# RWKV-7 and short-convolution mixer: keys too are placed by held GpSimd transfers, and the decayed reads move into the scan

## The chip, the cores and the metric

The kernel runs on one core of one Trainium2 chip. The metric is the device time of one launch, in microseconds (us), as the median over repeated runs. The engines are named as the profile names them: PE is TensorE (matrix products and transposes), DVE is VectorE, ACT is ScalarE, POOL is GpSimd, and SP starts most of the transfers.

## The reference

One layer of a diffusion backbone in fp32 with D_MODEL 2048: 128 context tokens, and 256 latent tokens that start from cached states. Both streams go through the same weights. One input projection `z = h @ w_in` feeds two branches. Branch B is a gated convolution of width 3. Branch A is RWKV-7 time mixing with 32 heads of size 64, in two directions; its scan is what the change touches:

```python
def step(S, inp):
    r_t, w_t, k_t, v_t, a_t, b_t = inp
    sa = jnp.einsum('dbhij,dbhj->dbhi', S, a_t)
    S = S * w_t[..., None, :] + sa[..., :, None] * b_t[..., None, :] + v_t[..., :, None] * k_t[..., None, :]
    y = jnp.einsum('dbhij,dbhj->dbhi', S, r_t)
    return S, y
...
S_fin, ys = _wkv_bidir(S0, _heads(r2), _heads(decay), _heads(k_dir), _heads(v2),
                       _heads(-kk2), _heads(kk2 * a))
y = ys[0] + ys[1]
mu = jnp.mean(y, axis=-1, keepdims=True)
var = jnp.mean(jnp.square(y - mu), axis=-1, keepdims=True)
y = ((y - mu) * lax.rsqrt(var + GN_EPS)).reshape(bsz, t, D_A) * lnx_g + lnx_b
```

A bonus from r, k and v is added, a gate is applied, and the two branches go through their output projections and are merged. Outputs are both token streams and the final context state of each direction.

## The kernel before

**Stages.** A prologue computes the conditioning and the normalised input. A loop over 16 blocks of two heads (128 channels) then runs branch A's scan. A tail projects the gated results out. Matrix products with weights are made in split precision: each weight and each activation is split into a high and a low part (`split`: ACT casts the high part, L88, DVE subtracts it for the low part, L89, named whi_ and wlo_ with a projection's letters), and `mm3` multiplies them in three products (L81 to L83).

**The stream.** The weight projections are cut into units, one `mm3` each with 384 tokens as columns. `Stream` holds them in order, loads their weights ahead, and `ds_.go(n)` puts the next n of them into PE's program. PE's order is exactly that of the code: a step of the scan, so many units, the next step. The numbers that set this are in one line of constants (PB0, PB1, H0, H1, CH0, CH1, WINDOW and others). The order on the other engines is set by a scheduler, which works with its own estimate of when each operand is ready, with priorities (the scan has one 300 higher), and with `issue_after`, which puts an instruction behind another.

**One block**, in the order of the code:

- *prep_b* (L668) makes the decayed keys `bk` (L680, L681) and the decayed reads `pr` (L682 and L685, L687) of the two directions, in tiles of 128 by 6 chunks by 128. After PB0 = 14 units come the masked products `pA` (L708), one burst of 24 small products for each direction, with PB1 = 6 units between; DVE masks them into the tile `A` (L714). GpSimd then multiplies `bk` by the decay of its chunk (L722), and DVE transposes the values v in 32x32 pieces into `vt` (L727). Pieces of A go through DRAM (`ui`, then `un` and `ux`) into a layout in which DVE solves 30 rows of a triangular system (L740, L742), and by `uo` back into A. DVE then transposes two pieces into `x11` (L755); the last of these is `box["turned"]`.
- *finish* of the block before (L948) stands between the PB0 units and the first masked product: PE transposes the normalised output `ytok` into `py`; ACT and DVE scale it, add the bonus and gate it.
- *prep_c* loads the initial state `s_in`. Eight GpSimd transfers (L777) carry `vt` into the lower half of `sav`. Ten PE transposes `pb` (L784) turn `bk`, and four ACT copies (L785) put them into `bt`, with one unit behind each group. Then the bonus's terms and the state's transposes.
- *prep_a* of the next block makes its decay and rates: the weights `lwh`, `lwl`, products `pl`, sigmoids `sig`, and the norm `kn` of its keys, held behind `box["turned"]`. Then the stream is filled up to WINDOW = 80 units (24 more in block 0, 16 more in block 15).
- *scan* starts with `pav` (L862), the corner products `pH` and `pX` with copies back into A and x11 (L890 for pX), and the bonus. Two chains of chunk steps then alternate, with CH0 = 2 units behind each step, CH1 = 4 when one is left. A step is: `po` from the state (L816), which adds to `sav` and `ytok`; `pq` (L833) with its copy into `sav` by ACT (L835); `pu` from `bt` and `sav` (L840), from which DVE writes the new state, by a copy in the first step of chain 0 (L843), by an addition otherwise (L845). At the end `py2` adds the rest of the output to ytok.
- *prep_k* of the next block (reciprocals L651, the product L652, scans L659, Exp of the decay `ep` on ACT L661, and the elementwise steps L664 to L666) is issued at a fixed place inside the scan, held behind two of the pX copies.
- *norm* (L932 to L942) makes the group norm of `ytok` on DVE, with a square on ACT and a power on GpSimd (L941).

Of the kernel before, what the change touches and what calls it, by code (L numbers as in the profile page):

```python
# [56 lines left out]
def hybrid_step(ctx, tc, cst, x_prompt, x_sample, state_f, state_b, c, c_ctx, ada_w, ada_b, norm_g,  # L57
# [613 lines left out]

    def prep_b(b, o):

        r, kk = r_[b], o["kk"]
        o["pr"], o["bk"] = [], []
        for d in range(2):
            ep, em, kd, bn = o["ep"][d], o["em"][d], o["kd"][d], o["bn"][d]
            pr = sp.tile([P, NCH, P], F32, tag=f"pr{d}", name=f"pr_{b}_{d}")
            bk = sp.tile([P, NCH, P], F32, tag=f"bk{d}", name=f"bk_{b}_{d}")
            V.tensor_tensor(bk[:, :, 0:C], c3(bn[:]), c3(em[:]), ALU.mult)  # L680
            V.tensor_tensor(bk[:, :, C:P], c3(kd[:]), c3(em[:]), ALU.mult)  # L681
            V.tensor_tensor(pr[:, :, 0:C], c3(kk[:, ::-1] if d else kk[:]), ep[:, :, 0:C], ALU.mult)  # L682
# [19 lines left out]
        for d in range(2):  # L702
# [7 lines left out]
            for n0, w in ((0, 4), (4, 2)):  # L710
                mk = cs[:, m0:m0 + P].rearrange("p (w t) -> p w t", t=C).unsqueeze(1).broadcast_to([P, w, 2, C])
                for h in range(2):
                    f0 = NCH * d + n0
                    last = V.tensor_tensor(A[:, :, f0:f0 + w, hss[h]].rearrange("p w n t -> p n w t"),  # L714
                                           pas[h, n0][:, 0:w, :].rearrange("p n (w t) -> p n w t", t=C), mk,
                                           ALU.mult).ins
# [4 lines left out]
        for d in range(2):
            G.tensor_tensor(o["bk"][d][:], o["bk"][d][:], o["ep"][d][:, :, C:C + 1].broadcast_to([P, NCH, P]), ALU.mult)  # L722

        vt = sp.tile([P, 2, T], F32, tag="vt", name=f"vt_{b}")
        with tc.issue_after(last):
            for d in range(2):
                V.transpose(vt[:, d], v_[b][:, ::-1] if d else v_[b][:])  # L727
# [25 lines left out]

        for d in range(2):
            box["turned"] = V.transpose(x11[0:32, 12 * d:12 * d + 12, :], blocks(A, d, 0)).ins  # L755

    def prep_c(b, o):
# [15 lines left out]

        x = o["vt"][:].rearrange("p d (n e t) -> p (d n) e t", e=2, t=32)
        for e in range(2):
            for q in range(4):
                G.dma_start(sav[C + 32 * e:C + 32 * e + 32, :, 32 * q:32 * q + 32], x[32 * q:32 * q + 32, :, e, :])  # L777
        yield 2
        for d in range(2):

            for n0, n1 in (((0, 4), (4, 5)), ((0, 3), (4, 6)))[d]:
                pb = bank(f"pb_{b}_{d}_{n0}")
                for n in range(n0, n1):
                    TE.transpose(pb[:, n - n0, :], o["bk"][d][:, n, :], ident)  # L784
# [11 lines left out]
    def scan(b, o):  # L796
# [7 lines left out]
        def chain(ch):  # L804
            ls = None
            for i in range((2, 4)[ch]):
# [30 lines left out]
                if need_state:  # L837
# [3 lines left out]
                    for hs in hss:  # L841
                        if zero:
                            V.tensor_copy(st[ch][hs, :, hs], pu[hs, 0:2, hs])  # L843
                        else:
                            V.tensor_tensor(st[ch][hs, :, hs], pu[hs, 0:2, hs], ls[hs, :, hs], ALU.add)  # L845
# [66 lines left out]
        yield 1  # L912
        V.tensor_tensor(ytok[:], ytok[:], py[:, 0:3, :], ALU.add)
# [12 lines left out]

    def norm(b, o):
# [4 lines left out]
        V.tensor_reduce(mu[:], y6, AX.X, ALU.add)  # L932
# [21 lines left out]

    def drive(gen, prio=0, at=None, fn=None):
        n = i = 0
        while True:
            if i == at:
                fn()
            i += 1  # L960
            with tc.high_priority(offset=prio):
# [4 lines left out]
            n += u
# [3 lines left out]
    drive(prep_a(0, cur))  # L970
    prep_k(0, cur)
    prev = None
    for b in range(NB):
# [17 lines left out]
        w = WINDOW + (FIRST if b == 0 else LAST if b == NB - 1 else 0)
# [192 lines left out]
```

## Time and profile before

| what | value |
|---|---|
| median of 3 runs | 2228.72 us (2228.09 to 2231.8) |
| the profiled execution's own time | 2230.84 us |
| its span in the trace | 2229.1 us |
| mean granted clock of TensorE | 0.996 |
| DVE busy | 1501.9 us (67%) |
| ACT busy | 978.4 us (44%) |
| POOL busy | 200.9 us (9%) |
| bytes moved | 347.88 MB, mean 156 GB/s |

The profile is of one execution, and the span is from its first to its last instruction. A row of the timeline gives start, duration, engine, line, operation, written tile and read tiles, shape and count; neighbouring equal instructions are one row, and a bracket says how long the engine was idle before and what ended it. A row of waits gives engine, tile and line that waited, the releaser, the total in us, the number and the longest. A row of windows gives the stretch, its length, each engine's busy time with its instructions (PE, weight loads, DVE, ACT, POOL), the granted clock, the busy share of the DMA engines, and GB/s.

### The profile page before, as it was taken

To read this page: it belongs to the slowest core of one execution; us is meant where nothing else is said; L and a number is where in the kernel's file an instruction comes from. 1 tells how busy PE (TensorE), PEld (TensorE's weight loads), DVE (VectorE), ACT (ScalarE), POOL (GpSimd) and SP (SyncE) were. 2 spreads that over 40 slices of the span, in tenths; PEclk is the share of its full clock that TensorE was granted. 3 is DMA by queue.
4 is the path that set the end of the run, shared out by engine and by line. 5 is a ranking of instruction groups with operands and counts; after the bars stand their busy time and mean duration, and the time that the engine had idled before them with its cause. 6 is when DMAs were issued, how large, how long until landed. Compare 5 with 4: busy or idle time off the path is not lost.

```text
span 2229.1 us, 40796 instructions
## 1 busy us (share of the span) xinstructions
PE 2168.6 (97%) x15924; PEld 2056.5 (92%) x15924; DVE 1501.9 (67%) x3288; ACT 978.4 (44%) x1704; POOL 200.9 (9%) x243
## 2 busy tenths in 40 slices
PE   6999999999999999999999999999999999999998
PEld 3588999999999999999999999999999999898988
DVE  3248567786877777868768786877777775444354
ACT  4245435453535454444436353536353634333333
POOL 2001010101010101111010101010101010000000
PEclk9999999999999999999999999999999999999999
DMA  9975464546464536364554546364546474887633
GB/s 337 346 213 131 142 144 128 126 108 146 107 147 107 133 108 143 112 144 105 138 115 128 126 108 146 108 145 124 138 121 153 147 206 146 292 273 234 219 132 114
DMA packets 480850, 347.88 MB, mean 156 GB/s; under 512 B 134720, under 2 KB 460944, under 8 KB 479760
## 3 DMA queue, kind: packets, MB, share of 16 engines
q1 hardware_dynamic: 475072, 337.20, 54.2%
q0 software_dynamic: 5152, 6.49, 2.0%
q8 instruction: 126, 2.06, 0.4%
q10 hardware_dynamic: 432, 1.57, 0.2%
q14 instruction: 68, 0.56, 0.1%
HBM read 312.09 MB, written 26.21 MB: 152 GB/s over the span
## 4 chain that ended last, share of the span: by engine, by line
PE 72%; DVE 13%; DMA 7%; ACT 3%; issue 2%; SPq 1%; POOL 0%; ACTq 0%; POOLq 0%; DVEq 0%
DMA raw_adah<-in_ada_w_dram 4%; PE d_rk L81 3%; PE d_rk L83 3%; PE d_rk L82 3%; PE d_gv L81 3%; PE d_gv L82 3%; PE d_gv L83 3%; PE pA L708 2%; PE d_oa L81 2%; PE d_oa L83 2%; PE d_oa L82 2%; PE d_bc L81 2%; PE d_mb L81 2%; PE d_gb L81 2%; PE d_mb L82 2%
## 5 line engine op out<-in xcount | busy, mean ns | idle before, releaser
L81 PE MATMUL d_rk<-h_hi,whi_rk 128*128 128x384 f32 x480 | 161.5, 337 | 0.6 <-ACT lst L554 0.6
L81 PE MATMUL d_gv<-h_hi,whi_gv 128*128 128x384 f32 x480 | 161.1, 336 | 0.0
L82 PE MATMUL d_gv<-h_lo,whi_gv 128*128 128x384 f32 x480 | 160.8, 335 | 0.0
L83 PE MATMUL d_gv<-h_hi,wlo_gv 128*128 128x384 f32 x480 | 160.7, 335 | 0.0
L83 PE MATMUL d_rk<-h_hi,wlo_rk 128*128 128x384 f32 x480 | 160.4, 334 | 0.0
L82 PE MATMUL d_rk<-h_lo,whi_rk 128*128 128x384 f32 x480 | 160.4, 334 | 0.0
L740 DVE TENSOR_TENSOR ut<-ux,un 112x30 f32<-112x30 f32 (+7 forms) x480 | 119.3, 248 | 16.6 <-DMA ux<-ui 4.2
L742 DVE TENSOR_TENSOR ux<-ux,ut 112x30 f32<-112x30 f32 (+7 forms) x480 | 119.3, 249 | 13.6
L88 ACT CAST whi_gv<-raw_gv 128x1024 fp32r<-128x1024 f32 (+1 forms) x64 | 64.0, 999 | 139.5 <-PE d_gv L82 34.0
L88 ACT CAST whi_rk<-raw_rk 128x1024 fp32r<-128x1024 f32 x60 | 62.9, 1052 | 119.1 <-PE d_rk L82 37.9
L89 DVE TENSOR_TENSOR wlo_rk<-raw_rk,whi_rk 128x1024 fp32r<-128x1024 f32 x60 | 73.1, 1221 | 50.0 <-ACT whi_rk L88 50.0
L81 PE MATMUL d_ob<-ybh,whi_ob 128*128 128x384 f32 x256 | 88.8, 347 | 3.8 <-ACT whi_ob L88 3.1
L81 PE MATMUL d_bg<-h_hi,whi_bg 128*128 128x384 f32 x256 | 91.8, 359 | 0.0
L81 PE MATMUL d_bc<-h_hi,whi_bc 128*128 128x384 f32 x256 | 91.7, 358 | 0.0
L81 PE MATMUL d_gb<-h_hi,whi_gb 128*128 128x384 f32 x256 | 91.7, 358 | 0.0
L81 PE MATMUL d_bx<-h_hi,whi_bx 128*128 128x384 f32 x256 | 91.5, 358 | 0.0
L81 PE MATMUL d_ma<-h_hi,whi_ma 128*128 128x384 f32 x256 | 91.0, 356 | 0.0
L81 PEld LDWEIGHTS d_rk<-h_hi,whi_rk 128*128 128x128 f32 x480 | 90.1, 188 | 0.9 <-ACT lst L554 0.9
L81 PEld LDWEIGHTS d_gv<-h_hi,whi_gv 128*128 128x128 f32 x480 | 90.4, 188 | 0.2
L82 PEld LDWEIGHTS d_gv<-h_lo,whi_gv 128*128 128x128 f32 x480 | 90.6, 189 | 0.0
L83 PEld LDWEIGHTS d_gv<-h_hi,wlo_gv 128*128 128x128 f32 x480 | 90.5, 188 | 0.0
L81 PE MATMUL d_mb<-h_hi,whi_mb 128*128 128x384 f32 x256 | 90.2, 352 | 0.0
(313 smaller groups left out, 6595.4 us busy)
## 6 DMA issues: line engine op xcount, KB each, us to landing
raw_adah<-in_ada_w_dram SPq DMA_DIRECT2D x64, 512.0 KB, 8.7
raw_rk<-in_w_in_dram SPq DMA_DIRECT2D x60, 512.0 KB, 5.3
raw_gv<-in_w_in_dram SPq DMA_DIRECT2D x60, 512.0 KB, 5.6
raw_ma<-in_w_in_dram SPq DMA_DIRECT2D x16, 1024.0 KB, 5.5
raw_mb<-in_w_in_dram SPq DMA_DIRECT2D x16, 1024.0 KB, 5.5
raw_bc<-in_w_in_dram SPq DMA_DIRECT2D x16, 1024.0 KB, 5.4
raw_bx<-in_w_in_dram SPq DMA_DIRECT2D x16, 1024.0 KB, 5.4
raw_bg<-in_w_in_dram SPq DMA_DIRECT2D x16, 1024.0 KB, 5.5
```

The lines of the kernel that those rows point to most:

```text
L81: TE.matmul(out, wh, xh, start=start, stop=False)
L82: TE.matmul(out, wh, xl, start=False, stop=False)
L83: TE.matmul(out, wl, xh, start=False, stop=stop)
L88: S.copy(hi[0:rows], src)
L89: V.tensor_tensor(lo[0:rows], src, hi[0:rows].bitcast(F32), ALU.subtract)
L708: TE.matmul(pas[h, n // 4 * 4][:, n % 4, :], bk[hss[h], n, :], pr[hss[h], n, :], start=True, stop=True)
L740: V.tensor_tensor(tv, ux[:, 0:m, s:s + 1].broadcast_to([112, m, w]), un[:, s:s + 1, s + 1:].broadcast_to([112, m, w]), ALU.mult)
L742: V.tensor_tensor(ux[:, 0:m, s + 1:], ux[:, 0:m, s + 1:], tv, ALU.add)
```

## The change

The lines are those of the new file where the rows are of after. Five things are changed.

1. *prep_b* is cut in three. The keys (`prep_p`) are made in the scan of the block before, directly behind prep_k; they are one tile for both directions now. The reads (`prep_r`) are made in that scan behind the first addition into chain 0's state, in two sets of tiles that alternate by block.
2. The PB0 units between `py2` and the first masked product are gone, so these are one burst on PE.
3. The keys are no longer turned on PE. DVE transposes `bk` in 32x32 pieces in place, and GpSimd moves the pieces into `bt` by 16 transfers. The eight transfers into `sav` become 16 of half the size. All 32 are held behind `mark`, a copy of one element of `ux` on GpSimd, which waits for the load of `ux`. In place of the ten transposes stands `yield 6`.
4. *norm* of a block moves from behind its scan to behind the next block's masked products, and *finish* with its `py` moves to NRM = 10 units behind these (16 units after the second product).
5. The transposes into `x11` are issued in the next block's prep_a, behind its second `lwl`. LAST goes from 16 to 30.

```diff
-    PRO, WINDOW, FIRST, LAST = 32, 80, 24, 16
+    PRO, WINDOW, FIRST, LAST, NRM = 32, 80, 24, 30, 10
...
+        if p is not None:
+            with tc.issue_after(lws):
+                p["turn_x"]()
...
+    def prep_p(b, o):
+
+        bks = sp.tile([P, 2, NCH, P], F32, tag="bk", name=f"bk_{b}")
+        o["bks"], o["bk"] = bks, [bks[:, d] for d in range(2)]
+        for d in range(2):
+            bk = o["bk"][d]
+            V.tensor_tensor(bk[:, :, 0:C], c3(o["bn"][d][:]), c3(o["em"][d][:]), ALU.mult)
+            V.tensor_tensor(bk[:, :, C:P], c3(o["kd"][d][:]), c3(o["em"][d][:]), ALU.mult)
...
-        yield PB0
...
+            o["masked"] = last
...
+            for d in range(2):
+                V.transpose(flat(o["bk"][d]), flat(o["bk"][d]))
...
+        mark = sp.tile([1, 1], F32, tag="mark", name=f"mark_{b}")
+        mark = G.tensor_copy(mark[:], ux[64:65, 0, 1:2]).ins
+        for d in range(2):
+            x = o["vt"][d][:].rearrange("p (n e t) -> p n e t", e=2, t=32)
+            for e in range(2):
+                for q in range(4):
+                    with tc.issue_after(mark):
+                        G.dma_start(sav[C + 32 * e:C + 32 * e + 32, NCH * d:NCH * d + NCH, 32 * q:32 * q + 32],
+                                    x[32 * q:32 * q + 32, :, e, :])
+        x = o["bks"][:].rearrange("p d n t -> p (d n) t")
+        for p in range(4):
             for q in range(4):
-                G.dma_start(sav[C + 32 * e:C + 32 * e + 32, :, 32 * q:32 * q + 32], x[32 * q:32 * q + 32, :, e, :])
-        yield 2
-        for d in range(2):
-
-            for n0, n1 in (((0, 4), (4, 5)), ((0, 3), (4, 6)))[d]:
-                pb = bank(f"pb_{b}_{d}_{n0}")
-                for n in range(n0, n1):
-                    TE.transpose(pb[:, n - n0, :], o["bk"][d][:, n, :], ident)
-                S.copy(bt[:, NCH * d + n0:NCH * d + n1, :], pb[:, 0:n1 - n0, :])
-                yield 1
+                with tc.issue_after(mark):
+                    G.dma_start(bt[32 * p:32 * p + 32, :, 32 * q:32 * q + 32],
+                                x[32 * q:32 * q + 32, :, 32 * p:32 * p + 32])
+        yield 6
...
+        for d in range(2):
+            ds_.go(next(pb_gen))
         if prev is not None:
+            norm(b - 1, prev, cur["masked"])
+        drive(pb_gen)
+        n = 0
+        if prev is not None:
+            ds_.go(NRM)
+            n = NRM
             finish(b - 1, prev)
...
+                prep_p(b + 1, nxt)
+
+        def reads():
+            with tc.issue_after(cur["st0"]):
+                prep_r(b + 1, nxt)
```

The order on DVE at the start of the scan of block 7, before: from the pX copy to the first state copy (names end in the block and a number; kn, sig, L, kd are the next block's, wlo_ is a weight split, st0 the state of chain 0).

```order
L890 COPY A_7_9660<-pX_7_10364 32x6x32 x2
L651 RECIPROCAL kn_8_10259<-kn_8_10259 128x128 x3
L659 SCALAR_TENSOR_TENSOR L_8_0_10409<-cs_74,sig_8_0_10200 128x384
L89 TENSOR_TENSOR wlo_bg4_0_1_10350<-raw_bg4_0_10343,whi_bg4_0_1_10349 128x1024
L843 COPY st0_1144<-pu_7_0_0_10447 64x2x64 x2
```

The same stretch after:

```order
L912 COPY A_7_9651<-pX_7_10444 32x6x32 x2
L657 RECIPROCAL kn_8_10337<-kn_8_10337 128x128 x3
L665 SCALAR_TENSOR_TENSOR L_8_0_10489<-cs_74,sig_8_0_10278 128x384
L658 SCALAR_TENSOR_TENSOR kn_8_10337<-kk_8_10242,kn_8_10337 128x384
L670 TENSOR_SCALAR kd_8_0_10493<-sig_8_2_10314,par_84,omka_136 128x384
L665 SCALAR_TENSOR_TENSOR L_8_1_10497<-cs_74,sig_8_1_10290 128x384
L671 TENSOR_TENSOR kd_8_0_10493<-k_8_10104,kd_8_0_10493 128x384
L672 TENSOR_TENSOR sig_8_2_10314<-kn_8_10337,sig_8_2_10314 128x384
L670 TENSOR_SCALAR kd_8_1_10501<-sig_8_3_10326,par_84,omka_136 128x384
L671 TENSOR_TENSOR kd_8_1_10501<-k_8_10104,kd_8_1_10501 128x384
L672 TENSOR_TENSOR sig_8_3_10326<-kn_8_10337,sig_8_3_10326 128x384
L864 COPY st0_1144<-pu_7_0_0_10532 64x2x64 x2
```

All of the next block's key preparation now stands ahead of the state copy, and one weight split less. In block 8 (as in the other even blocks from 2 to 12) four key products and a weight split stand there as well; DVE after, from the last kd on:

```order
L670 TENSOR_SCALAR kd_9_1_11665<-sig_9_3_11490,par_84,omka_136 128x384
L684 TENSOR_TENSOR bk_9_11669<-sig_9_2_11478,sig_9_0_11442 128x6x64
L671 TENSOR_TENSOR kd_9_1_11665<-k_9_11268,kd_9_1_11665 128x384
L672 TENSOR_TENSOR sig_9_3_11490<-kn_9_11501,sig_9_3_11490 128x384
L685 TENSOR_TENSOR bk_9_11669<-kd_9_0_11657,sig_9_0_11442 128x6x64
L684 TENSOR_TENSOR bk_9_11669<-sig_9_3_11490,sig_9_1_11454 128x6x64
L89 TENSOR_TENSOR wlo_bx5_0_1_11594<-raw_bx5_0_11587,whi_bx5_0_1_11593 128x1024
L685 TENSOR_TENSOR bk_9_11669<-kd_9_1_11665,sig_9_1_11454 128x6x64
L864 COPY st0_1144<-pu_8_0_0_11696 64x2x64 x2
```

The norm of block 7 on DVE, before, where it follows the scan with nothing between (mu and var are its statistics):

```order
L932 TENSOR_REDUCE mu_7_10731<-ytok_7_10261 128x6
L933 TENSOR_SCALAR mu_7_10731<-mu_7_10731 128x6
L934 TENSOR_TENSOR ytok_7_10261<-ytok_7_10261,mu_7_10731 128x384
L938 TENSOR_REDUCE var_7_10737<-ysq_7_10735 128x6
L939 TENSOR_SCALAR var_7_10737<-var_7_10737 128x6
L942 TENSOR_TENSOR ytok_7_10261<-ytok_7_10261,rs_7_10740 128x384
```

After, behind the masked products of block 8:

```order
L955 TENSOR_REDUCE mu_7_10900<-ytok_7_10341 128x6
L743 STREAM_TRANSPOSE bk_8_10505<-bk_8_10505 128x768
L89 TENSOR_TENSOR wlo_gb4_1_1_10839<-raw_gb4_1_10832,whi_gb4_1_1_10838 128x1024
L956 TENSOR_SCALAR mu_7_10900<-mu_7_10900 128x6
L743 STREAM_TRANSPOSE bk_8_10505<-bk_8_10505 128x768
L957 TENSOR_TENSOR ytok_7_10341<-ytok_7_10341,mu_7_10900 128x384
L741 STREAM_TRANSPOSE vt_8_0_10916<-v_8_10234 128x384
L741 STREAM_TRANSPOSE vt_8_1_10917<-v_8_10234 128x384
L961 TENSOR_REDUCE var_7_10906<-ysq_7_10904 128x6
L89 TENSOR_TENSOR wlo_rk9_0_0_11011<-raw_rk9_0_11007,whi_rk9_0_0_11010 128x1024
L962 TENSOR_SCALAR var_7_10906<-var_7_10906 128x6
L965 TENSOR_TENSOR ytok_7_10341<-ytok_7_10341,rs_7_10909 128x384
```

Four transposes and two weight splits now stand among the norm's steps. On ACT at the start of the scan of block 7, before (ep is the next block's decay, sav what pu reads, whi_ a weight cast):

```order
L890 COPY A_7_9660<-pX_7_10364 32x6x32 x2
L835 COPY sav_7_9841<-pq_7_0_0_10425 64x2x64 x2
L88 CAST whi_bg4_0_1_10349<-raw_bg4_0_10343 128x1024
L835 COPY sav_7_9841<-pq_7_1_0_10436 64x2x64 x2
L661 ACT_TABLE_LOAD
L661 ACTIVATE ep0_1148<-L_8_0_10409 128x6x64
```

After:

```order
L912 COPY A_7_9651<-pX_7_10444 32x6x32 x2
L667 ACT_TABLE_LOAD
L667 ACTIVATE ep0_1148<-L_8_0_10489 128x6x64
L856 COPY sav_7_9896<-pq_7_0_0_10510 64x2x64 x2
L856 COPY sav_7_9896<-pq_7_1_0_10521 64x2x64 x2
```

The table load and the first Exp now stand ahead of the copies from pq, and one weight cast less.

More of the change, by code (lines that the diff above doesn't have):

```diff
@@ L611, in hybrid_step, with prep_a @@
     G.memset(ux[:], 0.0)
-    def prep_a(b, o):
+    def prep_a(b, o, p=None):
         bs = slice(b * P, (b + 1) * P)
@@ L627, in prep_a @@
                 with tc.issue_after(box["kn"]) if m == 0 and "kn" in box else ExitStack():
-                    lwh, lwl = split(lraw[:], [96, 2, P], "lwh", "lwl", sp, f"{b}_{m}", rows=96)
+                    lwh = sp.tile([96, 2, P], F32R, tag="lwh", name=f"lwh_{b}_{m}")
+                    lwl = sp.tile([96, 2, P], F32R, tag="lwl", name=f"lwl_{b}_{m}")
+                    S.copy(lwh[:], lraw[:])
+                    lws = V.tensor_tensor(lwl[:], lraw[:], lwh[:].bitcast(F32), ALU.subtract).ins
                 yield 2
@@ L641, in prep_a @@
         kn = sp.tile([P, T], F32, tag="kn", name=f"kn_{b}")
-        with tc.issue_after(box["turned"]) if "turned" in box else ExitStack():
+        if p is not None:
+            with tc.issue_after(lws):
+                p["turn_x"]()
+        with tc.issue_after(box["turned"]) if p is not None else ExitStack():
             box["kn"] = V.tensor_scalar(kn[:], pn, 1e-24, None, ALU.max).ins
@@ L670, in prep_k, with prep_r @@
             o["bn"].append(aa)
-    def prep_b(b, o):
+    def prep_p(b, o):
[5 more added lines that the diff above has]
+            V.tensor_tensor(bk[:, :, C:P], c3(o["kd"][d][:]), c3(o["em"][d][:]), ALU.mult)
+    def prep_r(b, o):
         r, kk = r_[b], o["kk"]
-        o["pr"], o["bk"] = [], []
+        o["pr"] = []
         for d in range(2):
[L677 to L681, printed above, removed]
+            ep = o["ep"][d]
+            pr = sp.tile([P, NCH, P], F32, tag=f"pr{d}{b % 2}", name=f"pr_{b}_{d}")
             V.tensor_tensor(pr[:, :, 0:C], c3(kk[:, ::-1] if d else kk[:]), ep[:, :, 0:C], ALU.mult)
@@ L688, in prep_b @@
             o["pr"].append(pr)
-            o["bk"].append(bk)
-        yield PB0
+    def prep_b(b, o):
         def blocks(A, d, e):
@@ L721, in prep_b @@
         for d in range(2):
-            G.tensor_tensor(o["bk"][d][:], o["bk"][d][:], o["ep"][d][:, :, C:C + 1].broadcast_to([P, NCH, P]), ALU.mult)
-        vt = sp.tile([P, 2, T], F32, tag="vt", name=f"vt_{b}")
+            G.tensor_tensor(o["bk"][d], o["bk"][d], o["ep"][d][:, :, C:C + 1].broadcast_to([P, NCH, P]), ALU.mult)
+        vt = [tmp(f"vt_{b}_{d}") for d in range(2)]
         with tc.issue_after(last):
             for d in range(2):
-                V.transpose(vt[:, d], v_[b][:, ::-1] if d else v_[b][:])
+                V.transpose(vt[d][:], v_[b][:, ::-1] if d else v_[b][:])
+            for d in range(2):
+                V.transpose(flat(o["bk"][d]), flat(o["bk"][d]))
         o["vt"] = vt
@@ L752, in prep_b, with turn @@
                 nc.sync.dma_start(blocks(A, d, e), uo[d, e].rearrange("i s t -> s i t"))
-        for d in range(2):
-            box["turned"] = V.transpose(x11[0:32, 12 * d:12 * d + 12, :], blocks(A, d, 0)).ins
+        def turn():
+            for d in range(2):
+                box["turned"] = V.transpose(x11[0:32, 12 * d:12 * d + 12, :], blocks(A, d, 0)).ins
+        o["turn_x"] = turn
     def prep_c(b, o):
@@ L844, in chain @@
                         else:
[L845 removed]
+                            x = V.tensor_tensor(st[ch][hs, :, hs], pu[hs, 0:2, hs], ls[hs, :, hs], ALU.add)
+                            o[f"st{ch}"] = x.ins
                     yield 0
@@ L925, in scan, with norm @@
                                       nst[p0:p0 + 32, d, :].rearrange("i (b j) -> i b j", j=32))
-    def norm(b, o):
+    def norm(b, o, masked=None):
         ytok = o["ytok"]
@@ L931, in norm @@
         mu = sp.tile([P, 6], F32, tag="mu", name=f"mu_{b}")
-        V.tensor_reduce(mu[:], y6, AX.X, ALU.add)
+        with tc.issue_after(masked) if masked is not None else ExitStack():
+            V.tensor_reduce(mu[:], y6, AX.X, ALU.add)
         V.tensor_scalar(mu[:], mu[:], 1.0 / C, None, ALU.mult)
@@ L953, in finish, with drive @@
         nc.sync.dma_start(ya_d[b], ya[:])
-    def drive(gen, prio=0, at=None, fn=None):
-        n = i = 0
+    def drive(gen, prio=0, late=()):
+        n = 0
+        late = list(late)
         while True:
-            if i == at:
-                fn()
-            i += 1
+            for x in [x for x in late if x[0]()]:
+                x[1]()
+                late.remove(x)
             with tc.high_priority(offset=prio):
@@ L963, in drive @@
             if u is None:
+                assert not late
                 return n
@@ L971, in hybrid_step @@
     prep_k(0, cur)
+    prep_p(0, cur)
+    prep_r(0, cur)
+    ds_.go(PB0)
     prev = None
@@ L979, in hybrid_step @@
         pb_gen = prep_b(b, cur)
-        ds_.go(next(pb_gen))
+        for d in range(2):
+            ds_.go(next(pb_gen))
         if prev is not None:
+            norm(b - 1, prev, cur["masked"])
+        drive(pb_gen)
+        n = 0
+        if prev is not None:
+            ds_.go(NRM)
+            n = NRM
             finish(b - 1, prev)
-        drive(pb_gen)
-        n = drive(prep_c(b, cur))
+        n += drive(prep_c(b, cur))
         nxt = {}
+        w = WINDOW + (FIRST if b == 0 else LAST if b == NB - 1 else 0)
         if b < NB - 1:
@@ L989, in hybrid_step @@
                 n += 1
-            n += drive(prep_a(b + 1, nxt))
-        w = WINDOW + (FIRST if b == 0 else LAST if b == NB - 1 else 0)
+            n += drive(prep_a(b + 1, nxt, cur))
+        else:
+            cur["turn_x"]()
         if n < w:
@@ L998, in keys @@
                 prep_k(b + 1, nxt)
-        drive(scan(b, cur), 300, 3 if b < NB - 1 else None, keys)
-        norm(b, cur)
+                prep_p(b + 1, nxt)
+        def reads():
+            with tc.issue_after(cur["st0"]):
+                prep_r(b + 1, nxt)
+        late = ((lambda: all(cur.get("turn", (None,))), keys), (lambda: "st0" in cur, reads))
+        drive(scan(b, cur), 300, late if b < NB - 1 else ())
         prev, cur = cur, nxt
+    norm(NB - 1, prev)
     ds_.go(12)
```

7 lines of the change are left out of this document (2 added, 5 removed).

## The prediction

> **What bounds the kernel now.** I read the page first, then TensorE's waits, then one block of the scan loop by window and by timeline.
>
> ```profile
> span 2229.1 us, 40796 instructions
> ...
> PE 2168.6 (97%) x15924; PEld 2056.5 (92%) x15924; DVE 1501.9 (67%) x3288; ACT 978.4 (44%) x1704; POOL 200.9 (9%) x243
> ```
> ```profile
> PE pada L292 <- DMA raw_adah<-in_ada_w_dram: 21.7, 14, 9.7
> PE po L816 <- DVE st L845: 7.8, 9, 1.6
> ```
> ```profile
> 925.80:1030.10 104.30, 103.52 (x815) 101.22 (x814) 80.89 (x190) 47.80 (x89) 11.01 (x12) 1.00 0.51 126
> ```
>
> TensorE is the bound: busy 2168.6 of 2229.1 us. Its largest wait, 21.7 us, lies in the prologue, which the change leaves alone. In the 16 blocks its largest is po behind the state, 7.8 us in 9 places. The window is one whole block: 103.52 of 104.30 us busy, so 0.8 us of gaps. TensorE runs a written-out order, so this kernel gains only from work taken off TensorE, and it loses every microsecond by which another engine hands over late. VectorE is busy 80.89 of the same 104.30 us: it has room on average, but none is guaranteed at a given point.
>
> My sum is made against the profiled execution, 2230.8 us (span 2229.1 and 1.7 around it); the median of the runs is 2228.72, 2.1 lower. A difference of 0.2%, 4.5 us, is about what a measurement of this kernel can tell from none.
>
> **Taken away: the ten transposes of a block.**
>
> ```profile
> 946.36 0.33 PE L83 MATMUL d_bc<-h_hi,wlo_bc 128*128 128x384 f32 x1
> ...
> 948.96 0.34 PE L83 MATMUL d_bc<-h_hi,wlo_bc 128*128 128x384 f32 x1
> 949.13 0.60 PE L784 MATMUL pb<-cs,bk 128*128 128x128 f32 x4
> ...
> 951.58 0.38 PE L784 MATMUL pb<-cs,bk 128*128 128x128 f32 x2
> ...
> 952.15 0.34 PE L83 MATMUL d_rk<-h_hi,wlo_rk 128*128 128x384 f32 x1
> ```
>
> Five units lie between the first two rows: 2.60 us, so 0.52 each. From 948.96 to 952.15 are 3.19 us, holding four units (2.08) and all ten transposes. They cost 1.11 us a block; 16 blocks give **-17.8**. ScalarE's four copies of bt go too, worth nothing: it is busy 47.80 of 104.30 us. The number of stream units in a block stays 160, so the units that are moved cost nothing in themselves, and TensorE's interruptions by other work stay at three a block besides these.
>
> **The reads.** They were already made in the scan, four products behind a po:
>
> ```profile
> 923.81 0.56 DVE L682 TENSOR_TENSOR pr<-kk,ep 128x384 f32<-128x384 f32 x1 [1.70 <-PE po L816]
> ```
>
> VectorE waited 1.70 us before this one, so there is room, and they still follow the first state: 0.
>
> **The start of the scan.** The order of the changed program shows the next block's key preparation ahead of the first state copy on VectorE, in blocks 2 to 14; in blocks 0, 1 and 15 nothing moves there. Before, only the reciprocals, one scan and one weight split stand ahead of it:
>
> ```profile
> 1002.93 2.55 DVE L651 RECIPROCAL kn<-kn 128x128 f32<-128x128 f32 x3
> 1005.41 0.88 DVE L659 TENSOR_TENSOR_SCAN L<-cs,sig 128x384 f32<-128x384 f32 x1
> 1006.22 1.19 DVE L89 TENSOR_TENSOR wlo_bg<-raw_bg,whi_bg 128x1024 fp32r<-128x1024 f32 x1
> 1007.44 0.59 DVE L843 COPY st<-pu 64x128 f32<-64x128 f32 x2
> 1008.07 0.56 DVE L652 SCALAR_TENSOR_TENSOR kn<-kk,kn 128x384 f32<-128x384 f32 x1
> 1008.54 0.47 DVE L664 TENSOR_SCALAR kd<-sig,par,omka 128x384 f32<-128x384 f32 x1
> 1009.05 0.59 DVE L845 TENSOR_TENSOR st<-pu,ls 64x128 f32<-64x128 f32 x2
> ```
> ```profile
> 911.34 0.54 DVE L680 TENSOR_TENSOR bk<-sig,sig 128x384 f32<-128x384 f32 x1
> ...
> 914.75 0.59 DVE L845 TENSOR_TENSOR st<-pu,ls 64x128 f32<-64x128 f32 x2
> ```
> ```profile
> 1005.96 0.60 PE L840 MATMUL pu<-sav,bt 128*128 128x128 f32 x4
> ...
> 1008.94 0.61 PE L816 MATMUL po<-st,pr 128*128 128x128 f32 x4
> ```
> ```profile
> 915.48 0.68 PE L816 MATMUL po<-st,pr 128*128 128x128 f32 x4 [0.72 <-DVE st L845]
> ```
>
> Reciprocals to the scan are 2.48 us by starts, a scan to the next step 0.81, an elementwise step 0.47 to 0.51. A state ends at 915.34 and its po starts at 915.48, a hand-over of 0.14.
>
> Odd blocks, 3 to 13 and also 14, seven in all: 2.48, two scans (1.7), seven elementwise steps at 0.48 (3.4) make 7.5 us behind 1002.93. The copies then end at 1011.1, po could start at 1011.2, and TensorE would be there at 1008.94: **2.3 us late**. Even blocks 2 to 12, six: also four key products (the row at 911.34, 0.48 each by the step) and a weight split of 1.2, which is 3.1 more: **5.4 late**. 7 x 2.3 + 6 x 5.4 = **+48**. Ends: -8, if nothing is late and the 7.8 us of waits of before go, and 13 x 5.4 + 13 = +83, if the other chain's copies are each a microsecond late too. The middle is the sum of rows itself.
>
> ScalarE's part is inside this wait: the copy that pu waits for now stands behind a table load and an Exp.
>
> ```profile
> 1003.67 0.55 ACT L835 COPY sav<-pq 64x128 f32<-64x128 f32 x2 [1.06 <-PE pq L833]
> ...
> 1006.11 1.28 ACT L661 ACT_TABLE_LOAD   x1
> 1007.41 0.53 ACT L661 ACTIVATE ep<-L 128x384 f32<-128x384 f32 x1
> ```
>
> The Exp needs the scan's first result, 1006.3, and ends about 1006.9, so the copy is 3 us later and pu near 1007.5, not 1005.96. Of the 2.3 late, 1.5 would already show at pu; the total is set by the state.
>
> **The norm and py.** The previous block's norm now stands behind the masked products on VectorE, and py 16 units behind the second product on TensorE. Let X be that product's start, 943.32 here.
>
> ```profile
> 943.32 1.61 PE L708 MATMUL pA<-pr,bk 64*128 64x128 f32 x24
> ```
> ```profile
> 932.08 0.55 DVE L932 TENSOR_REDUCE mu<-ytok 128x6 f32<-128x384 f32 x1
> ...
> 934.94 0.17 DVE L939 TENSOR_SCALAR var<-var 128x6 f32<-128x6 f32 x1
> 936.64 0.56 DVE L942 TENSOR_TENSOR ytok<-ytok,rs 128x384 f32<-128x384 f32 x1 [1.53 <-POOL rs L941]
> ...
> 944.51 1.95 DVE L714 TENSOR_TENSOR A<-pA,cs 128x512 f32<-128x512 f32 x4 [0.77 <-PE pA L708]
> 946.38 1.03 DVE L727 STREAM_TRANSPOSE vt<-v 128x384 f32<-128x384 f32 x2
> ```
>
> The masked products end at X + 3.1 (944.51 + 1.95 - 943.32). Then, in the printed order: a reduction 0.55, the keys' two transposes (four times 128x384 at 0.52) 2.06, two weight splits 2.4, the mean 0.17, the subtraction 0.56 (as the row at 936.64), v's transposes 1.03, the second reduction 0.55, var to the final product with GpSimd's power between 1.70, that product 0.56: 9.6, less some 0.6 by which neighbouring rows of VectorE overlap. It ends at X + 12.2. TensorE is at py at X + 1.6 + 16 x 0.52 = X + 9.9. The wait is 2.3 us in 15 blocks: **+34**. Ends: 0, if the two splits (2.4) come later than the planner thinks, and 15 x 4 = +60, if GpSimd's power waits behind its two products on bk.
>
> **The clock.** Two places show what gaps of this size do.
>
> ```profile
> 171.90 0.51 PE L83 MATMUL pl<-l_hi,lwl 96*128 96x384 f32 x1 [1.66 <-DVE lwl L89]
> ```
> ```profile
> 169.00:172.00 3.00, 1.09 (x6) 0.44 (x4) 3.00 (x8) 2.46 (x5) 0.00 (x0) 1.00 0.00 0
> 172.00:176.00 4.00, 4.00 (x14) 4.00 (x15) 3.54 (x5) 1.24 (x3) 0.00 (x0) 0.57 0.85 249
> ```
>
> 1.9 us of gaps within 3 us, and the granted clock of the next 4 us is 0.57: 4 x 0.43 = 1.7 us lost beside the gap. The change gives 28 new waits (13 and 15) of 2.3 us or more; at most 28 x 1.7 = 48, at least 0. I take about half of the norm's (13) and three of the scan's (5): **+18**, since a gap just over 1.9 should do this only where it falls well. [...]
>
> **The transfers.** The mark waits until ux has landed, and then GpSimd issues 32 transfers: 16 halves of what eight made before for sav, and 16 for bt. Nothing else of this stretch is queued behind the mark.
>
> ```profile
> 947.99 4.95 POOL L777 DMA_DIRECT2D sav<-vt  x8 [1.40 <-ACT whi_rk L88]
> ...
> 958.65 0.17 DVE L745 TENSOR_SCALAR ux<-ux 48x16 f32<-48x16 f32 x1 [4.71 <-DMA ux<-ui]
> ```
> ```profile
> DMA to landing us min/median/max: 2.1/6.5/9.0
> ```
>
> ux is there at X + 15.3. An eight takes 4.95 to issue and 6.5 to land; four eights in line, 46 us, end at X + 61. The first pu stood at X + 62.6 and now stands at X + 72 (15 more units before the scan 7.8, py 0.5 and its wait 2.3, less 1.1): 10 us to spare, so 0. At 9.0 to land an eight takes 14, and they end at X + 71, just in time. The substitution's way home is covered better than before by the same 7.8 us.
>
> **Sum.** 2230.8 - 17.8 + 48 + 34 + 18 = 2313; less 2.1, **2311** for the median.
>
> **The rivals.** *F, the forecast*: state and norm both late, 2311. Its own range is 2280 (clock 0, norm's splits late) to 2338. Chance 0.63.
>
> *R1, only the scan is late.* For it: the splits of VectorE follow ScalarE's casts, which may come late, so that the norm's steps slip in ahead. Against: the two products on GpSimd can hold the power. 2230.8 - 17.8 + 48 + 6 (clock) - 2.1 = 2265. 0.10.
>
> *R2, only the norm is late.* For it: none of the rows, except that the reciprocals could begin earlier if pX does. 2230.8 - 17.8 + 34 + 10 - 2.1 = 2255. 0.07.
>
> *R3, neither is late: faster.* It decides at two points: the reciprocals to the state copy in 5.3 us (1008.94 - 0.14 - 0.59 - 1002.93), and the norm by X + 9.9. For it: average room on VectorE, 23 us a block. Then only the transposes count: 2230.8 - 17.8 - 2.1 = 2211, and 2203 without the old po waits. Against: the first point would need seven steps to take 2 us less than their rows. 0.10.
>
> *R4, the transfers are late too.* An eight above 14 us, while weight loads share the engines; each microsecond over costs 4 a block, 30 to 80 us on F with the clock: 2340 to 2390. 0.06.
>
> *Even*: a wait of about 1 us a block eats the gain: 2226 to 2232. 0.04.
>
> **How the numbers follow.** Likeliest is F, 2311. From 2250 to 2338 the range holds F, R1 and R2; R3, R4 and the even case, 0.20, are left out. Faster 0.10 (R3), same 0.04, slower 0.86 (F, R1, R2, R4).
>
> **What would show it.** In the profile after: no pb on TensorE; TensorE's waits with po behind st, or pu behind sav, near 48 us in 13 blocks, more in even ones; py behind ytok near 34 us in 15; windows at a granted clock of about 0.57 behind some of these. If VectorE's state copies start within 5.3 us of the reciprocals, the largest term is wrong; if py waits for nothing, the second; if the clock stays at 1.00 after gaps of 2 to 5 us, the third. If pu waits for bt or sav by transfer, it is R4.

## The result and the profile after

The changed kernel takes 2299.88 us (median of 4 runs, 2293.75 to 2300.66), the kernel before 2230.22 on the same occasion: ratio 1.0307, 95% interval 1.0286 to 1.0328. It is slower by 3.1%. The forecast was 2311.

The page of the profile after, its first lines:

```profile
span 2298.9 us, 41080 instructions
...
PE 2171.3 (94%) x15764; PEld 2051.6 (89%) x15764; DVE 1526.4 (66%) x3320; ACT 941.6 (41%) x1630; POOL 422.7 (18%) x643
```

TensorE executes 160 products fewer and yet is busy 2.7 us longer; its mean granted clock is 0.989, where it was 0.996, which is taken up below. Its idle time went from 60.5 to 127.6 us. TensorE's waits after, by tile and releaser:

```profile
PE py L971 <- DVE ytok L965: 25.9, 14, 1.9
...
PE pu L861 <- ACT sav L856: 21.6, 18, 2.3
PE d_ob L81 <- ACT ybh L508: 9.7, 3, 8.1
PE po L837 <- DVE st L864: 9.0, 11, 1.7
...
PE pX L876 <- issue: 4.0, 4, 1.5
PE po L837 <- DVE st L866: 3.4, 6, 0.9
PE pq L854 <- POOL A L897: 2.4, 5, 0.8
```

py behind the norm and pu and po in the scan are the two waits that the forecast named. The wait for ybh, and those of pX and pq, it did not name.

To see where the time went I cut each trace at two places of TensorE: from the first pav of a block to its first py2 ("scan", 52 units), and from there to the next block's pav ("rest", 108 units). Both hold the same stream units in both kernels. The stages are those of the profiled execution of each kernel.

| stage, after minus before | us |
|---|---|
| scan, 16 blocks | +43.5 |
| rest, blocks 0 to 13 | +19.6 |
| rest of block 14, up to block 15 | +9.1 |
| ahead of the blocks and behind them | -2.4 |
| span | +69.8 |

**The scan.** VectorE in block 7 (odd) and block 8 (even), the reciprocals and the first state copy:

```profile
1028.72 2.55 DVE L657 RECIPROCAL kn<-kn 128x128 f32<-128x128 f32 x3
...
1036.19 0.59 DVE L864 COPY st<-pu 64x128 f32<-64x128 f32 x2
...
1137.94 2.55 DVE L657 RECIPROCAL kn<-kn 128x128 f32<-128x128 f32 x3
...
1148.29 0.59 DVE L864 COPY st<-pu 64x128 f32<-64x128 f32 x2
```

and the po that follows each, on TensorE:

```profile
1036.93 0.68 PE L837 MATMUL po<-st,pr 128*128 128x128 f32 x4 [0.39 <-DVE st L864]
...
1149.03 0.68 PE L837 MATMUL po<-st,pr 128*128 128x128 f32 x4 [1.72 <-DVE st L864]
```

From reciprocals to copy it is 7.47 and 10.35 us; the forecast had 7.5 and 10.6, and before it was 4.51 (1007.44 - 1002.93). In these two blocks the reciprocals start 8.9 us behind pav in both kernels, so what came later lies between these two rows. Block 7's pav is at 1019.8 and block 8's at 1129.0, so po comes 17.1 and 20.0 us behind pav, where it was 14.95 before: 2.2 and 5.1 later. Over blocks 2 to 14 this adds up to 46.9 us.

**The norm.** VectorE's norm and TensorE's py around block 8's second masked product:

```profile
1068.84 1.95 DVE L727 TENSOR_TENSOR A<-pA,cs 128x512 f32<-128x512 f32 x4 [2.86 <-PE pA L721]
1070.71 0.54 DVE L955 TENSOR_REDUCE mu<-ytok 128x6 f32<-128x384 f32 x1
...
1078.96 0.56 DVE L965 TENSOR_TENSOR ytok<-ytok,rs 128x384 f32<-128x384 f32 x1 [1.46 <-POOL rs L964]
```
```profile
1067.65 1.61 PE L721 MATMUL pA<-pr,bk 64*128 64x128 f32 x24
...
1079.66 0.76 PE L971 MATMUL py<-cs,ytok 128*128 128x128 f32 x3 [1.87 <-DVE ytok L965]
```

With X at 1067.65, the norm ends at X + 11.9 (forecast 12.2) and py waits 1.87 us (forecast 2.3), nearly the same in 14 blocks.

**The transfers.** GpSimd between the masked products and the scan of block 8:

```profile
1113.22 0.17 POOL L793 COPY mark<-ux 1x1 f32<-1x1 f32 x1 [34.30 <-DVE ux L761]
1113.72 9.06 POOL L799 DMA_DIRECT2D sav<-vt  x16 [0.33 <-issue]
...
1135.11 1.83 POOL L805 DMA_DIRECT2D bt<-bk  x3 [1.61 <-DMA bt<-bk]
1136.98 1.38 POOL L897 MEMSET A<- 64x1536 f32 x1
```

The mark runs at X + 45.6, not at X + 15: the element of ux that it reads is on the diagonal, and the row says that it waits for VectorE's diagonal addition (L761). So the hold is not on the load of ux, as the list of changes and the prediction have it. All 32 are issued by X + 69.3, 8 us behind pav, and the scan's memset (L897) stands behind them. From the mark to there are 23.8 us. In blocks 2 to 14 this is alike, the mark between X + 43 and X + 46.

### The profile page after: what moved, and what is told of

It is laid out like the page before. It is cut to its first block, busy times and chain, and to the rows that moved or that the text cites. A ratio compares the mean times of both kernels' runs of the same rounds, so it can differ in the third digit from the quotient of the medians.

```text
span 2298.9 us, 41080 instructions
## 1 busy us (share of the span) xinstructions
PE 2171.3 (94%) x15764; PEld 2051.6 (89%) x15764; DVE 1526.4 (66%) x3320; ACT 941.6 (41%) x1630; POOL 422.7 (18%) x643
## 3 DMA queue, kind: packets, MB, share of 16 engines
q10 hardware_dynamic: 432, 1.57, 0.2%
## 5 line engine op out<-in xcount | busy, mean ns | idle before, releaser
L736 POOL TENSOR_TENSOR bk<-bk,ep 128x768 f32<-128x768 f32 x32 | 50.8, 1588 | 645.6 <-PE pA L721 557.8
L805 POOL DMA_DIRECT2D bt<-bk x256 | 156.1, 616 | 62.2 <-DMA bt<-bk 31.3
L799 POOL DMA_DIRECT2D sav<-vt x256 | 144.1, 571 | 14.1 <-issue 5.7
L756 DVE TENSOR_TENSOR ut<-ux,un 112x30 f32<-112x30 f32 (+7 forms) x480 | 119.5, 249 | 12.6 <-DMA ux<-ui 0.3
```

Source lines behind the costliest of these rows:

```text
L736: G.tensor_tensor(o["bk"][d], o["bk"][d], o["ep"][d][:, :, C:C + 1].broadcast_to([P, NCH, P]), ALU.mult)
L756: V.tensor_tensor(tv, ux[:, 0:m, s:s + 1].broadcast_to([112, m, w]), un[:, s:s + 1, s + 1:].broadcast_to([112, m, w]), ALU.mult)
L799: G.dma_start(sav[C + 32 * e:C + 32 * e + 32, NCH * d:NCH * d + NCH, 32 * q:32 * q + 32], x[32 * q:32 * q + 32, :, e, :])
L805: G.dma_start(bt[32 * p:32 * p + 32, :, 32 * q:32 * q + 32], x[32 * q:32 * q + 32, :, 32 * p:32 * p + 32])
```

## The experiments

All ratios are to the kernel before, with 95% intervals. The table gives the stages as above and the number of 3.4-us stretches at half clock (granted 0.50): inside blocks 0 to 13, and behind the ybh gap of block 14 (before has 0 and 0). Stages and stretches are of one profiled execution each, which can lie some us off the median (e8's took 2243.7 us).

| kernel | median us | ratio | scan | rest 0 to 13 | rest 14 | half-clock stretches |
|---|---|---|---|---|---|---|
| after | 2299.88 | 1.0307 (1.0286 to 1.0328) | +43.5 | +19.6 | +9.1 | 9 and 3 |
| e1_keys_held | 2264.65 | 1.0162 (1.0145 to 1.018) | +11.0 | +13.5 | +9.2 | 4 and 3 |
| e2_nrm14 | 2263.19 | 1.0161 (1.0146 to 1.0176) | +46.2 | -19.8 | +9.5 | 3 and 3 |
| e3_both | 2231.15 | 1.001 (1.0 to 1.0019) | +15.0 | -19.8 | +9.0 | 1 and 3 |
| e4_exp_held | 2298.09 | 1.0309 (1.0292 to 1.0326) | +43.9 | +19.6 | +8.6 | 14 and 2 |
| e5_nrm8 | 2306.5 | 1.0351 (1.0337 to 1.0365) | +26.4 | +40.5 | +8.8 | 11 and 3 |
| e6_both_yb | 2224.14 | 0.9984 (0.9976 to 0.9993) | +16.5 | -19.8 | +2.7 | 0 and 2 |
| e8_pe_turn | 2239.04 | 1.0047 (1.0033 to 1.006) | +5.4 | +2.0 | +9.1 | 0 and 3 |
| e9_mark_early | 2216.49 | 0.9948 (0.9935 to 0.996) | +5.2 | -19.8 | +3.2 | 0 and 2 |
| e10_mark_only | 2277.68 | 1.0228 (1.0212 to 1.0244) | +13.4 | +19.6 | +12.6 | 12 and 4 |
| e11_mark_nrm_yb | 2224.65 | 0.9988 (0.9979 to 0.9997) | +13.6 | -19.8 | +3.0 | 5 and 2 |

**e1_keys_held: the keys behind the first state copy.** prep_k yields after its reciprocals, and the rest of it and prep_p follow `first`, the copy into chain 0's state:

```diff
+            o["first"] = V.tensor_copy(st[ch][hs, :, hs], pu[hs, 0:2, hs]).ins
...
+        def keys2():
+            with tc.issue_after(cur["first"]):
+                for _ in rest[0]:
+                    pass
+                prep_p(b + 1, nxt)
```

> The next block's key preparation, all but the reciprocals, is held behind the first state copy of chain 0; all else is as after the change. My theory (VectorE's order at the start of the scan costs 43.5 us over the blocks): the scan stages go back to the 38 to 40 us of before, two lost clock windows go as well, 2255 to 2262 us. py still waits 1.9 us in 14 blocks. Rival (the 32 transfers are late or disturb the scan): the waits of pu and po stay, 2290 to 2305.

Measured 2264.65, 3 us above the range; the scan lost 32.5 of its 43.5 us. The waits of pu and po in it:

```profile
PE pu L862 <- ACT sav L857: 8.2, 9, 1.3
PE po L838 <- DVE st L867: 7.8, 9, 1.1
```

So holding the keys takes away three quarters of the scan term. The hold moves ScalarE's Exps too, since they need the keys' scans; e4 tells the two apart. po is back at the 7.8 of before; pu keeps 8.2, later in the scan, where the moved work now stands.

**e2_nrm14: py four units later.**

```diff
-    PRO, WINDOW, FIRST, LAST, NRM = 32, 80, 24, 30, 10
+    PRO, WINDOW, FIRST, LAST, NRM = 32, 80, 24, 30, 14
```

> py stands four stream units (2.1 us) later; the number of units in a block is unchanged. My theory (py waits 1.9 us for the norm in 14 blocks, 26 us, and 7 of the 10 lost clock windows of the blocks, 1.7 us each, follow these waits): py waits for nothing, the 7 windows go, 2258 to 2266 us. Rival (the clock windows have nothing to do with py's gaps): the waits go and the windows stay, 2270 to 2277. Rival (the wait is only handed on to the next place): 2295 or more.

2263.19, as the first theory says. py has gone from the list of waits, and so have the 7 half-clock stretches that followed it; in the scan there are three, where the changed kernel has two. The rest of a block is now 64.1 us, against 65.44 before the change.

**e3_both: both edits.** The sum of the two diffs above.

> Both edits at once: keys held behind the first state copy, and py four units later. My theory: the two terms add, what is left is the ten transposes a block saved (-17.8) and the late loads of yb in block 14 (8.1 us of wait and up to 5 of clock): 2218 to 2226 us, below the kernel before by 0.2 to 0.5%. Rival (the transfers or the merged burst cost something of their own): 2232 or more.

2231.15: the two terms add to within some 3 us (35 and 37 apart, 69 together), but 5 us more are left than I had said. The scan is 15.0 above before:

```profile
PE d_ob L81 <- ACT ybh L508: 9.2, 3, 7.6
PE pu L862 <- ACT sav L857: 8.2, 9, 1.3
...
PE pX L877 <- issue: 4.0, 4, 1.6
...
PE pq L855 <- POOL A L898: 2.3, 5, 0.6
```

pX and pq now point at the second rival, the transfers. e8 and e9 take that up.

**e4_exp_held: only ScalarE's Exps held.** The Exps move from prep_k to prep_p, which is issued behind the first two copies from pq; VectorE's other key steps stay ahead of the state copy.

```diff
+        for ep, L, sg in o["exps"]:
+            S.activation(ep[:, :, 1:C + 1], c3(L[:]), AF.Exp, scale=-DECAY)
+            S.activation(sg[:], L[:], AF.Exp, scale=DECAY)
...
+        def exps():
+            with tc.issue_after(cur["q"][0]), tc.issue_after(cur["q"][1]):
+                prep_p(b + 1, nxt)
```

> Only ScalarE's Exps of the next block's decay, and the key products that need them, are held behind the first two copies from pq; VectorE's other key steps stay ahead of the state copy (9 rows in odd blocks, 11 in even ones). My theory (VectorE's place of the state copy sets the wait, ScalarE's copies are inside it): pu's waits shrink, po's grow by as much in odd blocks, even blocks gain 1.9 us from the four products: 2285 to 2293 us. Rival (the copies from pq behind the table load and the Exp set it): the scan goes back to before, 2255 to 2265.

2298.09: above my range, and the rival is out by more than 30 us. The waits moved from pu to po and kept their sum:

```profile
PE po L839 <- DVE st L867: 30.0, 13, 3.2
...
PE pu L864 <- ACT sav L858: 0.6, 3, 0.2
```

So pu's 21.6 us were inside a wait that VectorE's state copy sets, as the prediction had it. The even blocks' 1.9 us came in full only in block 2 (a scan of +1.86 instead of +4.41 against before). In blocks 4, 6, 8 and 10 a half-clock stretch followed po's one wait of 2.5 to 3.2 us, and they gained 0.1 to 0.4; in block 12 none followed, and it gained 0.8.

**e5_nrm8: py two units earlier.** NRM = 8.

> The changed kernel with py two stream units (1.04 us) earlier, so that its gap is 2.9 us in place of 1.9 in 14 or 15 blocks; nothing else moves. My theory (about 1.9 us of idle TensorE in a stretch of 3.4 us costs a window of half clock, so 1.9 catches it in half the blocks and 2.9 in nearly all): 15 us of longer gaps and 6 to 8 more half-clock windows of 1.7 us, 2324 to 2331 us. [...]

2306.5, below the range. "Nothing else moves" was wrong: with the other constant the scheduler put VectorE's work at the start of the scan in another order (in block 7 the first state copy came 5.4 us behind the reciprocals, not 7.5), and the scan lost 17.1 us. In the rest, which the test was for, blocks 0 to 13 grew by 20.9: 14 x 1.04 = 14.6, and four more stretches at half clock. Half clock followed py's gap in 10 of the 14 blocks, where it had been 7: the clock followed the gap, in fewer blocks than I had thought. Two gaps of py of equal length (2.9 us), in windows of TensorE:

```profile
422.60:426.01 3.41, 1.90 (x11) 1.58 (x10) 2.49 (x5) 1.31 (x2) 0.68 (x1) 1.00 1.05 288
426.01:429.43 3.42, 2.00 (x13) 2.03 (x14) 1.30 (x3) 1.07 (x2) 0.68 (x1) 1.00 1.21 179
429.43:432.84 3.41, 3.41 (x21) 3.41 (x20) 2.53 (x5) 1.10 (x2) 0.00 (x0) 1.00 0.17 58
1081.40:1084.81 3.41, 0.50 (x5) 0.29 (x4) 1.55 (x3) 0.00 (x0) 1.35 (x1) 1.00 1.13 279
1084.81:1088.22 3.41, 3.41 (x14) 3.41 (x13) 1.50 (x3) 1.07 (x2) 0.00 (x0) 0.50 0.50 58
```

The first gap falls into two stretches, 1.5 and 1.4 idle in each, and the clock stays at 1.00. The second falls into one, 2.9 idle, and the next stretch runs at 0.50.

**e6_both_yb: e3, with the loads of yb ahead of those of ux.** On SP after the change the loads of yb, which the last projection needs, stand behind the load of ux, and TensorE waits for them:

```profile
1840.71 1.28 SPq L750 DMA_DIRECT2D ux<-ui  x2
1842.03 2.85 SPq L507 DMA_DIRECT2D yst_b<-yb_d  x5
```
```profile
1846.26 0.69 PE L81 MATMUL d_ob<-ybh,whi_ob 128*128 128x384 f32 x1 [8.12 <-ACT ybh L508]
```

Before, the first of them was issued at 1769.01, 7 us ahead of the product that needs it. The edit puts block 15's NRM units ahead of `drive(pb_gen)`:

```diff
+        if b == NB - 1:
+            ds_.go(NRM)
+            n = NRM
         drive(pb_gen)
```

> The kernel with both edits, and in block 15 the ten stream units ahead of py are put ahead of the loads of un and ux in the program, so that the loads of yb are issued before those of ux on SP; TensorE's order is the same. My theory (the 9 us of block 14 to 15 are the loads of yb queued behind those of ux, and the half clock after the gap): that stage loses 7 to 10 us, 2220 to 2226 us, faster than before by 0.2 to 0.5%. Rival (the loads wait for free buffers, or ux comes so late that the scan of block 15 waits): 2229 to 2240 us.

2224.14. The rest of block 14 lost 6.3 us, and of the 9.2 us of waits 3.7 are left. The loads of yb behind those of ux were the cause of most of this; they now start at 1773.12, directly behind a load of un, and the product follows at 1776.44. Why they start no earlier stays open.

**e8_pe_turn: the transposes back on TensorE.** e3 with the ten transposes and ScalarE's copies as before the change, without VectorE's transposes of bk and the 16 transfers into bt.

```diff
-                    G.dma_start(bt[32 * p:32 * p + 32, :, 32 * q:32 * q + 32],
-                                x[32 * q:32 * q + 32, :, 32 * p:32 * p + 32])
...
+                    TE.transpose(pb[:, n - n0, :], o["bk"][d][:, n, :], ident)
+                S.copy(bt[:, NCH * d + n0:NCH * d + n1, :], pb[:, 0:n1 - n0, :])
```

> The kernel with both edits, with the ten transposes of the keys put back on TensorE and their copies on ScalarE, and without VectorE's transposes of the keys and the 16 transfers into bt; the 16 transfers into sav stay. My theory (the transposes cost 1.11 us a block and the transfers nothing): 17 to 19 us above the kernel with both edits, 2247 to 2251 us. Rival (the transfers or VectorE's transposes cost what the transposes saved): 2229 to 2236 us.

2239.04, 8 us above e3 and not 17 to 19, and above the rival's 2236: both theories hold in part. In nine of blocks 1 to 13 the rest is 1.11 to 1.13 us longer, which is the price of the transposes (1.11 forecast); the other four are 2.1 to 3.2 us longer, and in these TensorE also waits 0.6 to 1.6 us for the weights lwh and lwl of the next block. But the scan is 9.6 us shorter: pX waits 0.3 us in all and pq not at all, and the half-clock stretch behind pX in block 13 is gone. This run took out the transfers into bt and VectorE's transposes at once; e9 leaves both in.

**e9_mark_early: the mark reads another element.** e6, and

```diff
-        mark = G.tensor_copy(mark[:], ux[64:65, 0, 1:2]).ins
+        mark = G.tensor_copy(mark[:], ux[64:65, 0, 0:1]).ins
```

> The kernel with both edits and the earlier loads of yb, and the mark reads element 0 of its row of ux in place of element 1, which the diagonal addition writes; so the mark is free when ux has landed, some 28 us earlier than in the changed kernel. VectorE's order at the start of the scan stays. My theory (the transfers, freed only 15 us ahead of the scan, run into it: pX and pq wait 7 to 9 us in all, partly behind the memset on GpSimd): these waits go, 2214 to 2219 us. Rival (the earlier transfers disturb the substitution or the weight loads as much): 2223 us or more.

2216.49, ratio 0.9948 (0.9935 to 0.996): faster than both kernels. The edit takes 7.7 us off e6. GpSimd in block 8 of this kernel, whose pav is at 1087.6:

```profile
1044.74 0.17 POOL L794 COPY mark<-ux 1x1 f32<-1x1 f32 x1 [3.56 <-DMA ux<-ui]
...
1068.72 0.61 POOL L806 DMA_DIRECT2D bt<-bk  x1 [1.89 <-DMA bt<-bk]
1089.32 1.38 POOL L898 MEMSET A<- 64x1536 f32 x1 [19.98 <-PE pav L885]
```

Now the mark does what its hold was said to do, and the transfers are issued 18 us ahead of pav. Of pX's wait 0.2 us is left, of pq's none, and the scan stages are those of e8 (+5.2 and +5.4). So the late transfers had cost them, not VectorE's transposes. The rival, that earlier transfers disturb something else as much, is out.

**e10_mark_only: that element alone in the changed kernel.**

> The changed kernel with that one element alone. The built order shows the first state copy of chain 0 back ahead of the next block's keys in all blocks, behind the reciprocals, one scan and one weight split, as before the change. My theory (the planner put the keys first because it had pu late, behind transfers held by the mark; so the scan's 43.5 us go, and the 6 us of pX and pq with them, while py still waits): 2245 to 2258 us. Rival (the order is right but pu waits for the transfers themselves, wherever they start): 2280 or more.

2277.68: the order on VectorE came back, the scan lost 30.1 us, and neither range was hit. Block 7:

```profile
1017.93 2.56 DVE L657 RECIPROCAL kn<-kn 128x128 f32<-128x128 f32 x3
...
1022.44 0.59 DVE L864 COPY st<-pu 64x128 f32<-64x128 f32 x2
```

From reciprocals to copy it is 4.51 us again, as before the change, and so in all of blocks 1 to 14. So the one element had moved VectorE's order too. That the scheduler had the transfers, and so pu, too late by its own estimate and filled the time with keys is my reading; no run shows its estimate. But the scan stays 13.4 above before, by a wait that I had not thought of:

```profile
PE py L971 <- DVE ytok L965: 25.8, 14, 1.9
...
PE d_gb L81 <- DVE bu L480: 6.1, 3, 2.0
PE d_bg L81 <- DVE bc L467: 6.0, 3, 2.0
```

d_gb and d_bg are stream units: their bank is freed by VectorE's step on an older projection (L467, L480), and ahead of that step VectorE now makes the key products that came into the scan. Each wait is 2.0 us, and five of the six are followed by a stretch at half clock.

**e11_mark_nrm_yb: the element, NRM 14 and the loads of yb, without the hold on the keys.**

> That one element, NRM 14 and the earlier loads of yb, and no hold on the keys. My theory: only the gains are left, 17.8 for the transposes and some of the yb gap (4 us of it stay): 2212 to 2219 us, faster than before by 0.4 to 0.8%. Rival (something of the merged burst or of the keys in the scan costs besides): 2224 or more.

2224.65, above my range, in the rival's: the same waits of d_gb and d_bg remain (6.1 us each), with five stretches at half clock. Against e9, which has the hold of e1 besides, that hold is worth 8 us.

## Why the prediction was right, point by point

- **Transposes, -17.8.** Right in mechanism and size. e8 measures 1.11 to 1.13 us a block. With the norm's wait gone (e2), the rest of a block is 1.32 shorter than before, so 0.2 us more than the transposes; that it is the merged burst was not tried by itself.
- **Scan, +48.** Right in the mechanism. State copies were late by what their rows add up to (7.47 and 10.35 us against 7.5 and 10.6), and the po behind them by 46.9 us over the 13 blocks. The stages grew by 43.5: before, most blocks had a po wait of 0.7 to 0.8 us later in the scan, and in the even blocks the late start swallowed it. e1, e4 and e10 show that VectorE's order, not ScalarE's Exps, set it.
- **Norm, +34.** Right in the mechanism; 25.9 in 14 blocks, not 34 in 15, since the chain ended at X + 11.9 and not 12.2, and TensorE came to py at X + 10.1 and not 9.9. e2 shows it by itself.
- **Clock, +18.** Right in the mechanism, and in the place: half clock followed py in 7 blocks and the scan's waits in two, where I had taken about half of 15 and three. The size came out smaller. The rest of a block is 67.74 us with a stretch behind py and 66.17 without, so 1.57 each and 11 us in all. The two in the scan cost 0.2 to 0.3 (blocks 6 and 10 take 43.06 and 43.14, blocks 4 and 8 without one 42.88 and 42.87): po waits for the state there anyway. Three more lie at the ybh gap, which I had not seen. A gap of 1.87 us that lay whole in one stretch was followed by half clock (the window from 1076.40, in the last section).
- **Transfers, 0.** This step failed. "The mark waits until ux has landed" (X + 15.3): it waited for the diagonal addition, at X + 43 to 46. "Nothing else of this stretch is queued behind the mark": the scan's memset is. The price was wrong as well, the other way: four eights were to take 46 us, and the 32 were issued in 23.8. That the two errors nearly cancelled is luck. pX and pq waited 6.4 us for this (4.0 and 2.4), but in the changed kernel little of it adds to the time: over blocks 2 to 14 the reciprocals start no later behind pav than before, and VectorE's keys hold po up behind them anyway. With the keys held it does, 7.7 us from e6 to e9. And e10 shows that the scan term, too, hangs on this element by way of the scheduler.
- **Not seen.** The loads of yb behind those of ux on SP: the stage grew by 9.1 us, and e6 takes 6.3 of it back. The forecast has no term for the order on SP.

Three terms came out too large: the scan by about 5 us, the norm by 8, the clock by 6 to 7. The ybh gap, which I had left out, gave 9 back. So that the sum is only 11 us off is in part luck. One bound does not follow from its own conditions either: with the clock at 0 and the norm's splits late, the terms give 2259, not the 2280 stated for F; the range as a whole began at 2250.

## What to carry to other kernels

Where a bound engine runs a fixed order, count what another engine does between the last thing that releases it and the first thing that it hands back; here that sum of rows told the wait to a few tenths of a microsecond. Look at what a hold really reads: one element more to the right, and 32 transfers waited for the end of a computation instead of for a load, and the scheduler moved other work by it. A change whose own gain is real (17.8 us here) can lose nearly five times that by the order that it brings along, and most of it is won back by mending the order: e9 is faster than both kernels.

## What the runs showed of the hardware

In the trace of the changed kernel the granted clock of TensorE is 0.50 in 13 stretches. The first begins at 35.31, and each of the others a whole number of times 3.413 us behind it: 44 times at 185.50, 306 at 1079.79, 529 at 1840.96. Eleven last 3.41 us, the one at 1840.96, behind the ybh gap, 10.24, and the last goes from 2294.94 to the end. In the trace of the kernel before there are five, which begin 0, 3, 41, 552 and 642 times 3.413 us behind 32.20. Windows of the changed kernel cut at these multiples, around two gaps of py of 1.88 and 1.87 us:

```profile
967.17:970.58 3.41, 2.98 (x18) 2.66 (x16) 2.54 (x5) 1.35 (x2) 0.64 (x1) 1.00 1.08 295
970.58:974.00 3.42, 1.97 (x13) 2.00 (x14) 1.27 (x3) 1.41 (x3) 0.71 (x1) 1.00 1.15 168
974.00:977.41 3.41, 3.41 (x21) 3.41 (x20) 2.10 (x5) 1.09 (x2) 0.00 (x0) 1.00 0.24 77
1076.40:1079.81 3.41, 1.54 (x10) 1.25 (x10) 1.65 (x3) 0.00 (x0) 1.35 (x1) 1.00 1.13 271
1079.81:1083.22 3.41, 3.41 (x13) 3.41 (x13) 1.53 (x4) 2.16 (x4) 0.00 (x0) 0.50 0.73 73
```

The first gap lies across a border, 0.4 us idle in one stretch and 1.5 in the next, and the clock stays at 1.00. The second lies in one stretch, and the next 3.41 us run at 0.50; the rest of that block takes 67.76 us, and 66.17 in the block of the first gap. I counted the idle time of TensorE in stretches cut like this from the first block's pav to the last one's in the two kernels and the ten experiments, leaving out stretches that were themselves at half clock: of those with 1.2 to 1.8 us idle 3 of 102 were followed by half clock, of those with 1.8 to 1.9 us 25 of 30, and of those with more all 40. Of some 5400 with less idle time one was (0.6 us, in e1), which stays unexplained. In the two kernels alone 18 stretches had 1.2 to 1.8 us idle, 1.76 at most, and none of them was followed by half clock; ten had 1.86 to 2.84, and all were. Whether a gap cost anything depended on where it fell: of the two gaps of 1.9 us above, and of the two of 2.9 us in e5, only the one that lay in a single stretch was followed by half clock. That fits with equal gaps of 1.88 us having cost the clock in 7 of 14 blocks.
